# Narrow products of an HGRN2 head in two groups instead of six or seven, with ScalarE copies of their operands

## The chip, the cores and the metric

The kernel runs on one core of a Trainium2 chip. The metric is the device time of one execution in microseconds (us): the median of repeated runs on the chip. Beside it stands one execution taken by the hardware profiler; every row below is from that one. TensorE is called PE here, VectorE DVE, ScalarE ACT, GpSimd POOL, and SyncE, which issues the DMAs, SP.

## The reference

Two layers of a hybrid decoder work on 512 prompt tokens and 8 samples of 4 tokens (T = 544 columns), width 1024. Layer 0 is block-sparse attention beside a convolution; the change leaves it as it is. Layer 1 is a gated linear recurrence (HGRN2) with 8 heads of 128 keys and 128 values:

```python
q, fz, i, g = _split(h @ w_in, C_SPLITS)
f = lb + (1.0 - lb) * jax.nn.sigmoid(fz.astype(jnp.float32))
kk = (1.0 - f)
qq = jax.nn.silu(q.astype(jnp.float32))
o, S = _hgrn2_scan(qq, kk, logf, vv, S0)
o = _rms(o, o_g)
return x + (o * jax.nn.silu(g)) @ w_out, S
...
decay = jnp.exp(jnp.where(causal, diff, -jnp.inf))
a = jnp.einsum('bhtk,bhsk,bhtsk->bhts', qc, kc, decay)
o = o_inter + jnp.einsum('bhts,bhsv->bhtv', a, vc)
S = (jnp.exp(b_last)[..., None] * S + jnp.einsum('bhsk,bhsv->bhkv', kc * jnp.exp(b_last - b), vc))
```

## The kernel before

**The wide part.** `proj(hd)` computes four column tiles of a head's projection (f and q, then v and the gate g), each in two halves of 272 columns. `unit` (lines 138 to 147) does one half: 8 blocks of the input by three passes (L142, L143, L144) that add the products of high and low parts into one PSUM bank, so 24 matmuls of 128x272 in a unit and 192 in a head: the wide matmuls. Weights come by SP's DMA into `wr`; ACT rounds them to the high part `wh` (L133) and DVE takes the remainder `wl` (L134). There are three banks with the tag "g". A unit needs one, and so waits until ACT or DVE has evacuated the unit three before it: f and v by ACT (L715, L736), q and the gate by ACT's sigmoid and a DVE product (L721 with L727, L732 with L733).

**The narrow part.** `scan(hd)` is the recurrence by doubling. On level hsz = 1, 2, ... 64 the older half of each block is multiplied with the younger half, and DVE then scales both by running products of f, in place. The products use only part of PE's array: 32x80 (L781, L783) from `qx` and `kk`, 32x56 (L823) from `qy` and `kk`, 16x16 (L839), 32x32 and 64x64 (L851) from `qq` and `kk`, and 32x128 (L910) from the samples' old state `S0`, which SP loads. Their results are copied by DVE (L786, L789, L827) and ACT (L843, L856) into the matrices AD, AS and AT. After that come transposes on PE (L102), the outputs `o` (L900, L902), their squares on ACT (L931, L933), a chain of short DVE steps that makes the inverse root (L109 to L115), the normed output `on` (L937), its five transposes, the gated product `gn` (L947), and its high and low parts `oh` (L105, ACT) and `ol` (L106, DVE), which the final projection reads.

**What sets the order.** The program is traced head by head (`drain`); heads 6 and 7 run side by side. A scheduler then moves each engine's instructions, so that on PE the narrow work of a head lies between wide matmuls of the next. Each engine takes its own list in order. `tc.issue_after` keeps instructions behind another one. Buffers with a tag are handed out in program order, and a new owner waits for the last reader of the old one. Tiles from `mtile` share 16 slots with the tag "m"; before, these hold `oh` and `ol` of the eight heads, while `gg` (the gate), `vT` (the raw values) and `gn` have buffers of their own.

Of the kernel before, what the change touches and what calls it, by code (L numbers as in the profile page):

```python
# [18 lines left out]
KT = 8  # L19
# [47 lines left out]
def hybrid_step(ctx, tc, xt_in, cache_kt, cache_v, conv_in, hgrn_in, page_table, par_in, k_norm_0,  # L67
# [595 lines left out]
    with tc.tile_pool(name="l1", bufs=1) as lp:  # L663
# [32 lines left out]
        oh = [mtile(("oh", k)) for k in range(KT)]  # L696
        ol = [mtile(("ol", k)) for k in range(KT)]
# [12 lines left out]
        def proj(hd):  # L710
            f, kk, qq = mk(lp, "f", [128, T], 2), mk(lp, "kk", [128, T], 2), mk(lp, "qq", [128, TP], 2)
            gg, vT = mk(lp, "gg", [128, T], 2), mk(lp, "vT", [128, T], 2)
# [4 lines left out]
            qx = mk(lp, "qx", [128, T // 32, 80], 1)  # L717
# [45 lines left out]
        def scan(hd, f, kk, qx, qq, vt, vs, vx, gg):  # L763
# [13 lines left out]
            pl = bank("s", 400)  # L777
            for c in range(4):
                for j in range(4):
                    t0 = c * 128 + j * 32  # L780
                    PE.matmul(pl[32 * j:32 * j + 32, c * 80:c * 80 + 80], kk[:, t0:t0 + 32], qx[:, t0 // 32],  # L781
                              start=True, stop=True, tile_position=(0, 32 * j))
            PE.matmul(pl[0:32, 320:400], kk[:, TP:T], qx[:, TP // 32], start=True, stop=True, tile_position=(0, 0))  # L783
            for l in range(4):
                m = lvm[:, 32 * l:32 * l + 32].rearrange("p (g t) -> p g t", t=4)[:, :, l:]
                V.copy_predicated(ad.rearrange("p c (g t) -> p c g t", t=4)[:, :, :, l:],  # L786
                                  m.unsqueeze(1).to_broadcast([128, 4, 8, 4 - l]),
                                  lag(pl[:, :320].rearrange("p (c x) -> p c x", c=4), l))
                V.copy_predicated(as_[:TS, :TS].rearrange("p (n g t) -> p n g t", n=1, t=4)[:, :, :, l:], m[:32].unsqueeze(1),  # L789
                                  lag(pl[:32, 320:400].unsqueeze(1), l))  # L790
# [10 lines left out]
            def quads(kk, tot):  # L801
                t4 = tot[:, :TP // 4].rearrange("p (n h j) -> p n h j", h=2, j=4)

                def by(l, j, n):
                    return t4[:, :, :, j:j + n].unsqueeze(4).to_broadcast([128, 16, 2, n, 4])

                q = qy[:, :16]
                for l in (2, 3):
                    n = 4 - l
                    V.tensor_tensor(blk_lag(q, l).rearrange("p n h (j t) -> p n h j t", t=4),  # L810
                                    blk_lag(q, l - 1)[:, :, :, 4:].rearrange("p n h (j t) -> p n h j t", t=4),
                                    by(l, 1, n), op=ALU.mult)
                qo = qq.rearrange("p (n h j t) -> p n h j t", h=2, j=4, t=4)
                qi = q[:, :, 0:32].rearrange("p n (h j t) -> p n h j t", h=2, t=4)
                G.tensor_copy(qo[:, :, :, 0], qi[:, :, :, 0])
                for l in range(1, 4):
                    V.tensor_tensor(qo[:, :, :, l], blk_lag(q, l)[:, :, :, 0:4],
                                    t4[:, :, :, 0:1].to_broadcast([128, 16, 2, 4]), op=ALU.mult)
                pl = bank("s", 224)
                for c in range(4):  # L820
                    for j in range(4):
                        t0 = c * 128 + j * 32
                        PE.matmul(pl[32 * j:32 * j + 32, c * 56:c * 56 + 56], kk[:, t0:t0 + 32], qy[:, t0 // 32],  # L823
                                  start=True, stop=True, tile_position=(0, 32 * j))
                for l in range(1, 4):
                    m = lvm[:, 32 * l + 96:32 * l + 128].rearrange("p (h x) -> p h x", h=2)[:, :, 4 * l:]
                    V.copy_predicated(ad.rearrange("p c (h x) -> p c h x", h=2)[:, :, :, 4 * l:],  # L827
                                      m.unsqueeze(1).to_broadcast([128, 4, 2, 16 - 4 * l]),
                                      blk_lag(pl.rearrange("p (c x) -> p c x", c=4), l))

            while hsz < 128:
                if hsz == 4:
                    quads(kk, tot)
                if hsz == 16:
                    pl = bank("s", 64)
                    for c in range(4):
                        for j in range(4):
                            s0 = c * 128 + j * 32
                            PE.matmul(pl[32 * j:32 * j + 16, c * 16:c * 16 + 16], kk[:, s0:s0 + 16], qq[:, s0 + 16:s0 + 32],  # L839
                                      start=True, stop=True, tile_position=(0, 32 * j))  # L840
                    for j in range(4):
                        r = slice(32 * j, 32 * j + 16)
                        A.activation(ad[r, :, 16:32], pl[r].rearrange("p (c t) -> p c t", c=4), AF.Copy)  # L843
                elif hsz > 16:
                    pl = bank("s")
                    nb, w = 128 // (2 * hsz), 2
                    for c in range(4):
                        for b2 in range(nb):
                            s0 = c * 128 + b2 * 2 * hsz
                            p0 = b2 * 64 + (c % w) * hsz  # L850
                            PE.matmul(pl[p0:p0 + hsz, c * hsz:(c + 1) * hsz], kk[:, s0:s0 + hsz],  # L851
                                      qq[:, s0 + hsz:s0 + 2 * hsz], start=True, stop=True, tile_position=(0, p0))
                    for b2 in range(nb):
                        for cw_ in range(w):
                            s0, p0 = b2 * 2 * hsz, b2 * 64 + cw_ * hsz
                            A.activation(at[s0:s0 + hsz, cw_::w, s0 + hsz:s0 + 2 * hsz],  # L856
                                         pl[p0:p0 + hsz, :4 * hsz].rearrange("p (c t) -> p c t", c=4)[:, cw_::w], AF.Copy)
# [45 lines left out]
            S0 = mk(lp, "S0", [128, NS, 128], 2)  # L903
            SP.dma_start(S0, hgrn_in[hd])
            pos = bank("s", 128)
            PE.matmul(pos, as_, vs, start=True, stop=False)
            p4 = bank("t", 128)
            for b2 in range(2):
                for j in range(4):
                    PE.matmul(p4[32 * j:32 * j + 32, :], qs[:, b2], S0[:, 2 * j + b2], start=(b2 == 0), stop=(b2 == 1),  # L910
                              tile_position=(0, 32 * j))
            c4 = mk(lp, "c4", [128, 128], 1)
            A.activation(c4, p4, AF.Copy)
# [26 lines left out]
            gn = mk(lp, "gn", [128, T], 1)  # L940
# [18 lines left out]
        for _ in range(4):  # L959
# [72 lines left out]
```

## Time and profile before

| | |
|---|---|
| time, median of 3 runs | 668.96 us (668.12 to 669.68) |
| the profiled execution: its time, its span | 672.1 us, 670.3 us |
| mean granted clock of PE | 0.987 |
| PE busy (share of the span) | 642.5 us (96%), 5806 instructions |
| PE weight loads busy | 584.0 us (87%) |
| DVE busy | 519.8 us (78%) |
| ACT busy | 350.9 us (52%) |
| POOL busy | 67.5 us (10%) |
| chain of work that ended last | PE 87%, DVE 6%, DMA 2%, ACT 2% |

The span runs from the first to the last instruction, and the execution's own time has 1.8 us around it. An engine's busy time counts overlapping instructions once. The chain is followed back from the last instruction, at each step to what released it. Layer 1 starts at about 345 us; its projections begin at 356.9 us.

### The profile page before, as it was taken

What the parts mean: (1) busy time and instruction counts of PE and PEld (TensorE: products, weight loads), DVE (VectorE), ACT (ScalarE), POOL (GpSimd) and SP (SyncE); (2) the same over time, 40 slices, a digit from 0 to 9 for tenths busy, and PEclk for the clock granted to TensorE, in tenths of its full rate; (3) what the DMA queues carried; (4) which work ended last, traced back from release to release, by engine and by line L of the source; (5) the groups of instructions that cost most, each with busy time, mean ns of one, the idle gap of its engine ahead of it and who ended that gap; (6) DMA issues with size and microseconds to landing.
All of it is one profiled execution on the core that took longest, in us unless ns stands there. A gap on an engine that the chain in (4) does not pass through costs nothing.

```text
span 670.3 us, 14835 instructions
## 1 busy us (share of the span) xinstructions
PE 642.5 (96%) x5806; PEld 584.0 (87%) x5806; DVE 519.8 (78%) x1238; ACT 350.9 (52%) x866; POOL 67.5 (10%) x95
## 2 busy tenths in 40 slices
PE   8799999979898999899998999999999999999997
PEld 6799999958777976557998999999999999999997
DVE  6999999899945974544896976978787878777656
ACT  7333445638557879533665455545454545435441
POOL 6000110000101100000001210202020202020100
PEclk8999999999989999999998999999999999999999
DMA  9421343121211060575453113141313131322114
GB/s 259 161 84 64 99 141 112 39 90 65 79 49 32 32 208 1 193 238 179 141 180 132 65 64 132 64 131 64 132 64 131 64 131 65 115 75 65 73 56 145
DMA packets 34583, 70.56 MB, mean 105 GB/s; under 512 B 7378, under 2 KB 16082, under 8 KB 34514
## 3 DMA queue, kind: packets, MB, share of 16 engines
q1 hardware_dynamic: 34514, 69.62, 31.7%
q8 instruction: 45, 0.74, 0.5%
q14 instruction: 24, 0.20, 0.1%
HBM read 59.88 MB, written 9.73 MB: 104 GB/s over the span
## 4 chain that ended last, share of the span: by engine, by line
PE 87%; DVE 6%; DMA 2%; ACT 2%; issue 1%; SPq 1%; POOL 0%; DVEq 0%
PE g L142 23%; PE g L144 22%; PE g L143 22%; PE t L102 4%; PE s L470 2%; DVE m L516 2%; PE o L493 1%; PE s L622 1%; DMA kn<-in_cache_kt_dram 1%; PE t L887 1%; PE o L900 1%; PE s L781 1%; PE o L902 1%; PE s L587 1%; DMA xTall<-in_xt_dram 1%
## 5 line engine op out<-in xcount | busy, mean ns | idle before, releaser
L142 PE MATMUL g<-h,wh 128*128 128x272 f32 x944 | 278.2, 295 | 8.5 <-ACT f L715 2.6
L143 PE MATMUL g<-h,wh 128*128 128x272 f32 x944 | 276.4, 293 | 2.0 <-DVE h L273 2.0
L144 PE MATMUL g<-h,wl 128*128 128x272 f32 x944 | 275.0, 292 | 0.0
L142 PEld LDWEIGHTS g<-h,wh 128*128 128x128 f32 x944 | 179.8, 191 | 12.8 <-ACT f L715 3.1
L143 PEld LDWEIGHTS g<-h,wh 128*128 128x128 f32 x944 | 179.6, 190 | 3.3 <-DVE h L273 2.5
L144 PEld LDWEIGHTS g<-h,wl 128*128 128x128 f32 x944 | 179.7, 190 | 1.1 <-issue 0.8
L133 ACT ACTIVATE wh<-wr 128x1024 fp32r<-128x1024 f32 (+4 forms) x90 | 88.2, 982 | 96.8 <-PE g L143 85.2
L134 DVE TENSOR_TENSOR wl<-wr,wh 128x1024 fp32r<-128x1024 f32 (+4 forms) x90 | 108.0, 1201 | 37.1 <-ACT wh L133 37.0
L516 DVE SCALAR_TENSOR_TENSOR m<-m,vecs,m 128x512 f32<-128x512 f32 x120 | 83.9, 732 | 0.1
L143 PE MATMUL g<-m,wh 128*128 128x272 f32 x256 | 74.3, 292 | 0.0
L142 PE MATMUL g<-m,wh 128*128 128x272 f32 x256 | 74.0, 298 | 0.1
L144 PE MATMUL g<-m,wl 128*128 128x272 f32 x256 | 74.0, 291 | 0.0
L142 PEld LDWEIGHTS g<-m,wh 128*128 128x128 f32 x256 | 47.5, 190 | 6.8 <-issue 3.6
L143 PEld LDWEIGHTS g<-m,wh 128*128 128x128 f32 x256 | 48.2, 188 | 2.2 <-DVE mx L598 0.8
L144 PEld LDWEIGHTS g<-m,wl 128*128 128x128 f32 x256 | 48.2, 188 | 0.4 <-issue 0.2
L478 DVE TENSOR_REDUCE mx<-s 128x1 f32<-128x128 f32 (+3 forms) x32 | 15.4, 482 | 15.5 <-PE s L472 15.5
L470 PE MATMUL s<-kz,qT 128*128 128x128 f32 (+3 forms) x64 | 23.5, 451 | 0.3 <-ACT PP L481 0.2
L916 ACT ACTIVATE S<-S,tot 128x128 f32<-128x128 f32 x64 | 20.4, 390 | 4.8 <-PE t L910 4.8
L865 DVE TENSOR_TENSOR kk<-kk,tot 128x256 f32<-128x256 f32 (+1 forms) x48 | 21.8, 454 | 0.0
L918 POOL TENSOR_TENSOR ve<-vx,cst 128x1024 fp32r<-128x1024 f32 x8 | 15.5, 1942 | 62.4 <-DVE vx L708 45.5
L971 DVE TENSOR_TENSOR xTall<-g,xTall 128x272 f32<-128x272 f32 x32 | 13.4, 436 | 8.4 <-PE g L144 8.0
L481 ACT ACTIVATE PP<-s,mx,rq 128x128 f32<-128x128 f32 (+3 forms) x32 | 19.6, 612 | 0.2
(292 smaller groups left out, 981.6 us busy)
## 6 DMA issues: line engine op xcount, KB each, us to landing
wr<-in_w_in_dram SPq DMA_DIRECT2D x58, 512.0 KB, 3.5
wr<-in_w_out_dram SPq DMA_DIRECT2D x16, 512.0 KB, 3.6
kn<-in_cache_kt_dram SPq DMA_DIRECT2D x16, 256.0 KB, 3.3
kn<-in_cache_v_dram SPq DMA_DIRECT2D x16, 256.0 KB, 4.3
S<-in_hgrn_dram SPq DMA_DIRECT2D x8, 512.0 KB, 3.6
out_hgrns_dram<-S SPq DMA_DIRECT2D x8, 512.0 KB, 3.3
xTall<-in_xt_dram SPq DMA_DIRECT2D x8, 272.0 KB, 5.4
out_y_dram<-xTall SPq DMA_DIRECT2D x8, 272.0 KB, 2.1
```

The source lines that it names most:

```text
L102: PE.transpose(out, in_, ident[:np_, :np_])
L133: A.activation(wh, raw, AF.Copy)
L134: V.tensor_tensor(wl, raw, wh, op=ALU.subtract)
L142: PE.matmul(ps, wh[:, k - k0, :], ah, start=(k == k0), stop=False)
L143: PE.matmul(ps, wh[:, k - k0, :], al, start=False, stop=False)
L144: PE.matmul(ps, wl[:, k - k0, :], ah, start=False, stop=(k == k1 - 1))
L470: PE.matmul(ss[hh][:, :L], qT[:, i * 128:(i + 1) * 128], kT[:, hh, 0:L], start=True, stop=False)
L481: A.activation(P[:, :L], s[:, :L], AF.Exp, bias=mx[:, 1:2], scale=rqc, accum_out=mx[:, 2:3])
L516: V.scalar_tensor_tensor(cy[c][:, :TP], up[c][:, j:j + TP], cw[:, c, j:j + 1], cy[c][:, :TP], op0=ALU.mult, op1=ALU.add)
L865: V.tensor_tensor(k3[:, :, 0, :], k3[:, :, 0, :], t3[:, :, 1:2].to_broadcast([128, nblk, hsz]), op=ALU.mult)
L916: A.activation(S0[:, n], S0[:, n], AF.Copy, scale=tots[:, n:n + 1])
L918: G.tensor_tensor(ve, vx.unsqueeze(1).to_broadcast([128, NS, 128]), exm.unsqueeze(2).to_broadcast([128, NS, 128]), op=ALU.mult)
```

## The change

Narrow products: a head has two groups now. The first, at hsz = 4 (L810 to L831), holds the 32x56 products (L818), behind them the 32x80 products (L824, L826) and the products with the old state (L829). The second, at hsz = 64 (L855 to L872), holds the 64x64 (L859), the 32x32 (L865) and the 16x16 products (L869). Operands that have been overwritten by then are kept by ACT copies with the tag "kv" (two buffers): 1-f of 544 columns (L783), and for hsz 16 and 32 the older half of `kk` and the younger half of `qq`, 256 columns each (L851, L852): five copies in a head, 40 in all. `qx` has two buffers, and `S0` is loaded before the first group (L780). The heads 6 and 7 are joined after six steps of head 6 instead of four.

Buffers: `gg` and `vT` come from the 16 slots "m"; `gn` is written over `gg` (L960); `oh` and `ol` are taken for a head when it is done, that of the last head from the tag "f".

```diff
-        oh = [mtile(("oh", k)) for k in range(KT)]
-        ol = [mtile(("ol", k)) for k in range(KT)]
+        oh, ol = [None] * KT, [None] * KT
...
-            gg, vT = mk(lp, "gg", [128, T], 2), mk(lp, "vT", [128, T], 2)
+            gg, vT = mtile(("gg", hd), F32), mtile(("vT", hd), F32)
-            qx = mk(lp, "qx", [128, T // 32, 80], 1)
+            qx = mk(lp, "qx", [128, T // 32, 80], 2)
...
+            S0 = mk(lp, "S0", [128, NS, 128], 2)
+            SP.dma_start(S0, hgrn_in[hd])
+            c4 = mk(lp, "c4", [128, 128], 1)
+            kv = mk(lp, "kv", [128, T], 2)
+            A.activation(kv, f, AF.Copy, scale=-1.0, bias=1.0)
+            def behind(ins):
+                return tc.issue_after(ins.ins)
...
                 pl = bank("s", 224)
+                pf = bank("s", 400)
+                p4 = bank("t", 128)
-                        PE.matmul(pl[...], kk[:, t0:t0 + 32], qy[:, t0 // 32], ...)
+                        last = PE.matmul(pl[...], kk[:, t0:t0 + 32], qy[:, t0 // 32], ...)
+                with behind(last):
+                            PE.matmul(pf[...], kv[:, t0:t0 + 32], qx[:, t0 // 32], ...)
+                    PE.matmul(pf[0:32, 320:400], kv[:, TP:T], qx[:, TP // 32], ...)
+                            PE.matmul(p4[...], qs[:, b2], S0[:, 2 * j + b2], ...)
+                A.activation(c4, p4, AF.Copy)
...
+                if hsz in (16, 32):
+                    old = mk(lp, "kv", [128, T], 2)[:, :TP].rearrange("p (a n t) -> p a n t", a=2, t=hsz)
+                    A.activation(old[:, 0], kk[...][:, :, 0], AF.Copy)
+                    A.activation(old[:, 1], qq[...][:, :, 1], AF.Copy)
+                    olds.append(old)
+                if hsz == 64:
+                    k16, k32 = olds
+                            last = PE.matmul(pl[...], kk[:, s0:s0 + 64], qq[:, s0 + 64:s0 + 128], ...)
+                    with behind(last):
+                                PE.matmul(pl[...], k32[:, 0, 2 * c + b2], k32[:, 1, 2 * c + b2], ...)
+                                PE.matmul(pl[...], k16[:, 0, 4 * c + j], k16[:, 1, 4 * c + j], ...)
...
-                V.scalar_tensor_tensor(gn[:, sl], p, vec("on"), gg[:, sl], op0=ALU.mult, op1=ALU.mult)
+                V.scalar_tensor_tensor(gg[:, sl], p, vec("on"), gg[:, sl], op0=ALU.mult, op1=ALU.mult)
+            oh[hd] = mtile(("oh", hd))
+            ol[hd] = mtile(("ol", hd)) if hd < KT - 1 else mk(lp, "f", [128, T], 2, F32R)
             for sl in (slice(0, 256), slice(256, T)):
-                split(oh[hd][:, sl], ol[hd][:, sl], gn[:, sl])
+                split(oh[hd][:, sl], ol[hd][:, sl], gg[:, sl])
...
-        for _ in range(4):
+        for _ in range(6):
             next(s6)
```

**Place A, the end of head 0.** PE before: `o_4739` is head 0's output, `s_5132` takes head 1's first products, `t_4804` and `t_4809` the transposes of head 0's normed output; g are wide matmuls. Left out are wide matmuls alone, in the first gap 30 of them and in the second 21.

```order
L902 MATMUL o_4739<-S_4733,qq_4279 128x128
L922 MATMUL t_4776<-ve_4771,kts_4721 128x512
L823 MATMUL s_5132<-qy_5087,kk_4819 32x56 x16
L144 MATMUL g_5363<-h_81,wl_5334 128x272
...
L839 MATMUL s_5158<-qq_4820,kk_4819 16x16 x16
...
L142 MATMUL g_5418<-h_83,wh_5333 128x272
L102 MATMUL t_4804<-cst,on_4799 128x128 x4
L102 MATMUL t_4809<-cst,ons_4800 128x128
L143 MATMUL g_5418<-h_91,wh_5333 128x272
```

PE now (`o_4742`, `s_5102`, `t_4793` and `t_4798` are the same things):

```order
L925 MATMUL o_4742<-S_4736,qq_4263 128x128
L143 MATMUL g_5003<-h_95,wh_4939 128x272
L144 MATMUL g_5003<-h_87,wl_4940 128x272
L818 MATMUL s_5102<-qy_5078,kk_4810 32x56 x16
L102 MATMUL t_4793<-cst,on_4789 128x128 x4
L102 MATMUL t_4798<-cst,ons_4790 128x128
L824 MATMUL s_5103<-qx_4814,kv_5088 32x80 x16
L826 MATMUL s_5103<-qx_4814,kv_5088 32x80
L142 MATMUL g_5029<-h_80,wh_4945 128x272
```

The transposes of the normed output stood 59 rows behind the last output matmul; now two wide matmuls and the first products stand between them. On ACT the list there is now (`sq` and `sd`: the norm's squares and sums of head 0; `m_4264` is the gated output, `m_4813` head 1's raw values, which L735 evacuates from a wide bank):

```order
L852 ACTIVATE kv_5164<-qq_4811 128x256
L947 ACTIVATE sq_4770,sd_4771<-o_4742 128x128
L133 ACTIVATE wh_5331<-wr_5329 128x1024
L947 ACTIVATE sq_4770,sd_4771<-o_4742 128x128 x3
L851 ACTIVATE kv_5164<-kk_4810 128x256
L105 ACTIVATE m_4803<-m_4264 128x256
L735 ACTIVATE m_4813<-g_4949 128x272
L735 ACTIVATE m_4813<-g_5003 128x272
```

A weight rounding (L133) stands between the first and the other three squares.

**Place B, heads 2 to 5, here where head 3 ends while head 4 is projected.** PE before: first products, transposes of head 3's output, 16x16 products with transposes between them, 32x32 products, each between wide matmuls (only wide ones are left out, but for the last transpose of the output):

```order
L144 MATMUL g_6866<-h_86,wl_6837 128x272
L823 MATMUL s_6635<-qy_6590,kk_6322 32x56 x16
L142 MATMUL g_6866<-h_87,wh_6836 128x272
...
L142 MATMUL g_6895<-h_81,wh_6830 128x272
L102 MATMUL t_6307<-cst,on_6302 128x128 x4
...
L144 MATMUL g_6895<-h_86,wl_6831 128x272
L839 MATMUL s_6661<-qq_6323,kk_6322 16x16 x9
L102 MATMUL t_6572<-cst,vT_6325 128x128 x4
L102 MATMUL t_6581<-cst,r_6579 128x128
L839 MATMUL s_6661<-qq_6323,kk_6322 16x16 x7
...
L144 MATMUL g_6921<-h_87,wl_6837 128x272
L851 MATMUL s_6686<-qq_6323,kk_6322 32x32 x8
L142 MATMUL g_6962<-h_80,wh_6952 128x272
```

PE now: the first group with the five transposes inside, and the second group.

```order
L144 MATMUL g_6527<-h_87,wl_6464 128x272
L818 MATMUL s_6626<-qy_6602,kk_6334 32x56 x16
L102 MATMUL t_6317<-cst,on_6313 128x128 x4
L102 MATMUL t_6322<-cst,ons_6314 128x128
L824 MATMUL s_6627<-qx_6338,kv_6612 32x80 x16
L826 MATMUL s_6627<-qx_6338,kv_6612 32x80
L142 MATMUL g_6553<-h_80,wh_6469 128x272
...
L143 MATMUL g_6859<-h_92,wh_6849 128x272
L859 MATMUL s_6702<-qq_6335,kk_6334 64x64 x4
L865 MATMUL s_6702<-kv_6695 32x32 x8
L829 MATMUL t_6628<-S_6609,QS_4245 32x128 x8
L869 MATMUL s_6702<-kv_6688 16x16 x16
L927 MATMUL s_6782<-VS_4244,AS_4243 128x128
```

Products that stood apart stand together; the wide matmul behind L826, `g_6553`, is the first of a unit, and its bank is the one of `g_6473`.

**Place C, the same place on ACT and DVE.** ACT before (`gn` to `m` is the output rounding, `vT` the evacuation of the values):

```order
L133 ACTIVATE wh_6836<-wr_6834 128x1024
L736 ACTIVATE vT_6325<-g_6515 128x272
L916 ACTIVATE S_6250<-S_6250,tot_6126 128x128 x6
...
L931 ACTIVATE sq_6283,sd_6284<-s_6252 128x128
L933 ACTIVATE sq_6283,sd_6284<-o_6242 128x128 x4
L715 ACTIVATE f_6822<-g_6840 128x272
L721 ACTIVATE sg_6891<-g_6866 128x272
L105 ACTIVATE m_4264<-gn_6306 128x256
L105 ACTIVATE m_4264<-gn_6306 128x288
```

ACT now (`m_6327` is head 3's `oh`, `m_5828` its gated output, `m_6337` head 4's raw values, from the banks `g_6473` and `g_6527`):

```order
L852 ACTIVATE kv_6688<-qq_6335 128x256
L133 ACTIVATE wh_6855<-wr_6853 128x1024
L105 ACTIVATE m_6327<-m_5828 128x256
L735 ACTIVATE m_6337<-g_6473 128x272
L735 ACTIVATE m_6337<-g_6527 128x272
L105 ACTIVATE m_6327<-m_5828 128x288
```

DVE now (`m_5828` is the gated output again, `wl_6856` the remainder of `wh_6855`):

```order
L888 TENSOR_TENSOR kk_6334<-kk_6334,tot_6618 128x64x4
L134 TENSOR_TENSOR wl_6856<-wr_6853,wh_6855 128x1024
L960 SCALAR_TENSOR_TENSOR m_5828<-t_6317,vecs,m_5828 128x256 x2
L960 SCALAR_TENSOR_TENSOR m_5828<-t_6322,vecs,m_5828 128x32
L888 TENSOR_TENSOR kk_6334<-kk_6334,tot_6683 128x32x8
```

The evacuation of the values stood ten rows ahead of the output rounding, and stands directly behind its first piece now; the piece reads what DVE writes behind the remainder of the weights that ACT rounded one row earlier.

## Rows read from the trace of the kernel before

**Rows 1.** Windows view, projections of layer 1: busy time (count) by engine, PEclk, DMA.

```profile
365.00:656.00 291.00, 291.00 (x3171) 275.92 (x3170) 223.34 (x663) 141.15 (x430) 37.64 (x46) 1.00 0.26 87
```

**Rows 2.** Timeline, PE: start, us, line; narrow stretches alone, then two joined.

```profile
480.27 0.29 PE L144 MATMUL g<-h,wl 128*128 128x272 f32 x1
480.49 0.60 PE L823 MATMUL s<-qy,kk 128*32 128x56 f32 x32
481.25 0.29 PE L143 MATMUL g<-h,wh 128*128 128x272 f32 x1
...
455.84 0.33 PE L851 MATMUL s<-qq,kk 128*32 128x32 f32 x16
456.33 0.29 PE L143 MATMUL g<-h,wh 128*128 128x272 f32 x1
...
641.93 0.64 PE L910 MATMUL t<-S,QS 128*32 128x128 f32 x16
642.73 0.29 PE L142 MATMUL g<-m,wh 128*128 128x272 f32 x1
...
619.06 0.64 PE L910 MATMUL t<-S,QS 128*32 128x128 f32 x16
619.52 0.31 PE L851 MATMUL s<-qq,kk 128*32 128x32 f32 x16
619.99 0.29 PE L142 MATMUL g<-m,wh 128*128 128x272 f32 x1
```

**Rows 3.** Timeline, PE: 64-wide products alone, then joined to the first products.

```profile
625.14 0.45 PE L851 MATMUL s<-qq,kk 128*64 128x64 f32 x8
625.76 0.29 PE L142 MATMUL g<-m,wh 128*128 128x272 f32 x1
...
611.32 0.45 PE L851 MATMUL s<-qq,kk 128*64 128x64 f32 x8
611.71 0.60 PE L823 MATMUL s<-qy,kk 128*32 128x56 f32 x32
612.47 0.29 PE L143 MATMUL g<-m,wh 128*128 128x272 f32 x1
```

**Rows 4.** Timeline, ACT: a weight rounding, two norm squares, an output rounding.

```profile
487.33 1.06 ACT L133 ACTIVATE wh<-wr 128x1024 fp32r<-128x1024 f32 x1
...
474.51 0.28 ACT L933 ACTIVATE sq<-o 128x128 f32<-128x128 f32 x1
474.91 0.28 ACT L933 ACTIVATE sq<-o 128x128 f32<-128x128 f32 x1
...
483.16 0.42 ACT L105 ACTIVATE m<-gn 128x256 fp32r<-128x256 f32 x1 [1.06 <-DVE gn L947]
```

**Rows 5.** Timeline, DVE: a weight remainder, three steps of the root, gated product.

```profile
526.79 1.21 DVE L134 TENSOR_TENSOR wl<-wr,wh 128x1024 fp32r<-128x1024 f32 x1
...
476.20 0.15 DVE L109 TENSOR_SCALAR sd<-sd 128x5 f32<-128x5 f32 x1
477.52 0.14 DVE L114 SCALAR_TENSOR_TENSOR sd<-sd 128x5 f32<-128x5 f32 x1
479.11 0.69 DVE L937 TENSOR_TENSOR on<-o,sd 128x512 f32<-128x512 f32 x1
...
482.65 0.48 DVE L947 SCALAR_TENSOR_TENSOR gn<-t,vecs,gg 128x256 f32<-128x256 f32 x1
```

**Rows 6.** Windows view: three idle stretches of PE, each with what followed.

```profile
171.80:176.00 4.20, 2.71 (x22) 2.67 (x22) 4.15 (x10) 3.70 (x7) 0.00 (x0) 1.00 0.00 0
...
183.20:185.80 2.60, 0.82 (x7) 0.53 (x6) 1.80 (x4) 1.64 (x3) 0.00 (x0) 1.00 0.41 156
185.80:188.60 2.80, 2.80 (x12) 2.80 (x13) 2.44 (x5) 0.00 (x0) 0.00 (x0) 0.50 0.36 100
...
354.20:356.90 2.70, 0.05 (x2) 0.01 (x1) 2.52 (x5) 2.67 (x5) 2.15 (x12) 0.92 0.57 164
356.90:359.60 2.70, 2.70 (x12) 2.70 (x13) 2.14 (x7) 1.73 (x3) 0.00 (x0) 0.50 0.90 338
```

More of the change, by code (lines that the diff above doesn't have):

```diff
@@ L776, in scan @@
                 V.tensor_tensor(q4[:, :, :, l], lag(qx, l)[:, :, :, 0], f4[:, :, :, 0], op=ALU.mult)
[L777 to L790, printed above, removed]
             for b2 in range(2):
@@ L822, in quads @@
                         t0 = c * 128 + j * 32
-                        PE.matmul(pl[32 * j:32 * j + 32, c * 56:c * 56 + 56], kk[:, t0:t0 + 32], qy[:, t0 // 32],
-                                  start=True, stop=True, tile_position=(0, 32 * j))
+                        last = PE.matmul(pl[32 * j:32 * j + 32, c * 56:c * 56 + 56], kk[:, t0:t0 + 32], qy[:, t0 // 32],
+                                         start=True, stop=True, tile_position=(0, 32 * j))
+                with behind(last):
+                    for c in range(4):
+                        for j in range(4):
+                            t0 = c * 128 + j * 32
+                            PE.matmul(pf[32 * j:32 * j + 32, c * 80:c * 80 + 80], kv[:, t0:t0 + 32], qx[:, t0 // 32],
+                                      start=True, stop=True, tile_position=(0, 32 * j))
+                    PE.matmul(pf[0:32, 320:400], kv[:, TP:T], qx[:, TP // 32], start=True, stop=True, tile_position=(0, 0))
+                    for b2 in range(2):
+                        for j in range(4):
+                            PE.matmul(p4[32 * j:32 * j + 32, :], qs[:, b2], S0[:, 2 * j + b2], start=(b2 == 0),
+                                      stop=(b2 == 1), tile_position=(0, 32 * j))
+                A.activation(c4, p4, AF.Copy)
+                for l in range(4):
+                    m = lvm[:, 32 * l:32 * l + 32].rearrange("p (g t) -> p g t", t=4)[:, :, l:]
+                    V.copy_predicated(ad.rearrange("p c (g t) -> p c g t", t=4)[:, :, :, l:],
+                                      m.unsqueeze(1).to_broadcast([128, 4, 8, 4 - l]),
+                                      lag(pf[:, :320].rearrange("p (c x) -> p c x", c=4), l))
+                    V.copy_predicated(as_[:TS, :TS].rearrange("p (n g t) -> p n g t", n=1, t=4)[:, :, :, l:], m[:32].unsqueeze(1),
+                                      lag(pf[:32, 320:400].unsqueeze(1), l))
                 for l in range(1, 4):
@@ L833, in scan @@
                     quads(kk, tot)
-                if hsz == 16:
-                    pl = bank("s", 64)
-                    for c in range(4):
[L837 to L840, printed above, removed]
+                if hsz in (16, 32):
+                    old = mk(lp, "kv", [128, T], 2)[:, :TP].rearrange("p (a n t) -> p a n t", a=2, t=hsz)
+                    A.activation(old[:, 0], kk[:, :TP].rearrange("p (n s t) -> p n s t", s=2, t=hsz)[:, :, 0], AF.Copy)
+                    A.activation(old[:, 1], qq.rearrange("p (n s t) -> p n s t", s=2, t=hsz)[:, :, 1], AF.Copy)
+                    olds.append(old)
@@ new lines, in scan @@
+                if hsz == 64:
+                    k16, k32 = olds
+                    pl = bank("s")
+                    for c in range(4):
+                        s0, p0 = c * 128, (c % 2) * 64
+                        last = PE.matmul(pl[p0:p0 + 64, 192 + c * 64:256 + c * 64], kk[:, s0:s0 + 64],
+                                         qq[:, s0 + 64:s0 + 128], start=True, stop=True, tile_position=(0, p0))
+                    with behind(last):
+                        for c in range(4):
+                            for b2 in range(2):
+                                p0 = b2 * 64 + (c % 2) * 32
+                                PE.matmul(pl[p0:p0 + 32, 64 + c * 32:96 + c * 32], k32[:, 0, 2 * c + b2],
+                                          k32[:, 1, 2 * c + b2], start=True, stop=True, tile_position=(0, p0))
+                        for c in range(4):
+                            for j in range(4):
+                                PE.matmul(pl[32 * j:32 * j + 16, c * 16:c * 16 + 16], k16[:, 0, 4 * c + j],
+                                          k16[:, 1, 4 * c + j], start=True, stop=True, tile_position=(0, 32 * j))
@@ L841, in scan @@
                     for j in range(4):
                         r = slice(32 * j, 32 * j + 16)
[L843 to L857, printed above, removed]
+                        A.activation(ad[r, :, 16:32], pl[r, :64].rearrange("p (c t) -> p c t", c=4), AF.Copy)
@@ new lines, in scan @@
+                    for hz, o in ((32, 64), (64, 192)):
+                        for b2 in range(64 // hz):
+                            for cw_ in range(2):
+                                s0, p0 = b2 * 2 * hz, b2 * 64 + cw_ * hz
+                                A.activation(at[s0:s0 + hz, cw_::2, s0 + hz:s0 + 2 * hz],
+                                             pl[p0:p0 + hz, o:o + 4 * hz].rearrange("p (c t) -> p c t", c=4)[:, cw_::2],
+                                             AF.Copy)
@@ L902, in scan @@
                     PE.matmul(po[:, sl], qq[:, sl], S[:, (c - 1) * 128:c * 128], start=False, stop=True)
-            S0 = mk(lp, "S0", [128, NS, 128], 2)
-            SP.dma_start(S0, hgrn_in[hd])
             pos = bank("s", 128)
             PE.matmul(pos, as_, vs, start=True, stop=False)
[L907 to L913, printed above, removed]
             PE.matmul(pos, cst[:, C_SEL2:C_SEL2 + 128], c4, start=False, stop=True)
```

2 lines of the change are left out of this document (1 added, 1 removed).

## The prediction

> **What bounds the kernel now.** I read the views in this order: busy time by stage, PE's timeline where narrow products stand, the rows of ACT and DVE that would lie in the new chains, and PE's idle stretches with the clock behind them. In the projections of layer 1 PE is busy for 291.00 of 291 us, at the full clock [rows 1]. DVE has 223 us of work there, ACT 141, POOL 38, and the DMA engines are busy for 0.26. So whatever PE is spared here is gained, as long as nothing else makes it wait; no row of this stage has PE waiting, so every wait that the change adds is paid in full. Layer 0 keeps its order on every engine.
>
> **What the grouping saves.** A wide matmul takes about 0.125 us: 22 of them in 2.71 us of work at full clock [rows 6]. A narrow stretch costs more than its own products, since PE goes over to it and back. From the last wide start to the narrow start there are 0.22 us (480.27 to 480.49) [rows 2]. From the narrow start to the second wide start behind it there are 0.49 us for the 32x32 products, 0.80 for those with the old state, and 0.93 for both in one stretch. Less the two wide cadences that lie in each of these distances (0.25), the first two cost 0.46 and 0.77, 1.23 together, and the joined stretch 0.90: a join at the same width saves 0.33. Where the width changes inside the stretch, 64 wide and then 32 wide, the same sum is 0.59 and 0.73 apart, against 0.73 + 0.39 = 1.12 joined [rows 2, 3]: a join saves 0.20 there, so the change of width keeps 0.13.
>
> By the order of layer 1, 58 narrow stretches become 32, and the changes of width inside a stretch go from one to eight. That is 26 x 0.33 - 7 x 0.13 = 7.7 us less on PE. If each change of width ate the whole saving, it would be 19 x 0.33 = 6.3; if it ate nothing, 8.6. I take 7.7, as measured, and keep both ends. The Trainium skill (TensorEngine Tiling (Array Packing), Key Properties) says that a change of tiling mode, not just of tile, drains TensorE, which would make every change of width cost like a return to the wide matmuls; by that rule alone the saving is the lower end, 6.3. The trace agrees that a change of width costs something, but shows 0.13, less than half of 0.33.
>
> **What is added at nothing.** 40 ACT copies: 32 of 256 columns, 0.42 each as the output rounding of that size [rows 4], and 8 of 544, about twice that: 20 us of ACT beside its 141 in 291. They are hidden, but for what stands behind them in ACT's list; the chains below contain that. `S0` is loaded earlier, ahead of two weight loads on SP, with DMA busy for 0.26; and `qx` has a second buffer, so the earlier product of the next head needs no wait. The second group waits for DVE's scaling up to hsz = 32; between the two groups lie 38 wide matmuls, 4.7 us, and the 1.9 of the first group itself, beside about as much DVE work. I put no wait there, with 0 to 1 us per head as bounds: this is the thinnest cover.
>
> **The new wait at the end of head 0 (place A).** PE now has the transposes of head 0's output directly behind head 1's first products, which start two wide matmuls after the last output product. Count from the start of these products. ACT has done the first square; then comes a weight rounding of 1.06, and the other three squares at 0.40 each (474.51 to 474.91) [rows 4]: 2.3 us. DVE takes the weight remainder of 1.21 meanwhile. The chain of short steps took 2.9 from its first step to the start of the normed output, of which 1.6 are the eight steps from 477.52 on; other copies lay between the first three [rows 5]. I take 2.5 (2.2 without anything between, 2.9 as seen). The normed output takes 0.69. So the transposes can start at 2.3 + 0.1 + 2.5 + 0.7 = 5.6, and PE is through the first products at 0.5: it waits 5.1 us. In the order of before 53 wide matmuls behind the first products, 6.6 us, covered this. Behind the transposes the chain of the next paragraph adds 0.5: 5.6 us in all, 5.2 to 6.2.
>
> **The new wait in heads 3 to 6 (places B, C).** The unit behind L826 needs the bank of the values' first half. ACT evacuates that bank behind the first piece of the previous head's output rounding, and ACT takes its list in order. That piece needs the gated product, which on DVE stands behind the remainder of weights that ACT rounds last before, and ACT can start that rounding only when the unit ahead of the first products is through, since its buffer is still read until then. Counted again from the start of the first products: rounding 1.06, remainder 1.21, gated product 0.48, output rounding 0.42 [rows 4, 5], evacuation about the same 0.4, less some overlap: 3.5. PE has, until then, the first products (0.5), five transposes at no more than a wide one's 0.125 (0.6), and 17 products of 80 columns with the return, as the 16 of 128 (0.8) [rows 2]: 1.9. It waits 1.6 us, 1.3 to 2.0. The order is alike in the projections of heads 3, 4, 5 and 6: 6.4 us. For head 2 the remainder stands behind the gated product, the wait is about 0.2. Before, the evacuation stood ten rows ahead of the output rounding, and no row showed the wait.
>
> **The clock.** PE idle for 2.7 us was followed by 2.7 us at a granted clock of 0.50, which is 1.2 instead of 2.4 GHz: 12 wide matmuls in place of 21 [rows 6], 1.35 us lost. The wait of 5.1 us should do this once. After 1.6 us with little work the clock stayed at 1.00 (171.80 to 176.00); after 2.6 us with 0.82 busy it fell to 0.50. The waits of 1.6 lie behind a second and more of narrow work and transposes, between these two rows; I take no fall there.
>
> **The sum.** -7.7 + 5.6 + 0.2 + 6.4 + 1.35 = +5.9 us. The profiled execution took 672.1 us, with a span of 670.3, so it would be 678.0 there; the median of the runs shown is 3.1 lower, and on it I forecast 668.96 + 5.9 = 674.9. About 0.2%, 1.3 us, is what a measurement of this kernel can tell from no change.
>
> **The rivals.**
> - *The clock falls in heads 3 to 6 too.* For it speaks the window with 0.82 of 2.6 us busy [rows 6]; against it, that narrow products keep PE busy here. It adds 4 x 1.35 = 5.4: 680.3. A chance of 0.2.
> - *Only the wait at the end of head 0 bites.* If the values are evacuated in time in heads 3 to 6 (the rounding of the weights starting earlier than its list and buffer let me read), 6.4 us go: 668.5, no change. 0.08.
> - *No new wait: faster.* If the chains behind both waits end before PE is through, only the saving is left: 668.96 - 7.7 = 661.3. For it speaks that DVE and ACT have idle time in every head [rows 1]. It decides at place A: the chain would have to end within 0.5 us of the first products instead of 5.6, which needs the squares to run well ahead of them; the list of ACT speaks against it, since the last output matmul comes only two wide ones before. 0.07.
> - *DVE is late for the second group*, by about 1 us in six heads: 681. 0.07. It looks like the forecast with one more wait per head.
> - The forecast itself, with the bounds of its terms (671 to 678): 0.58.
>
> **How the numbers follow.** The likeliest is 674.9. The range takes the forecast's bounds and most of the clock's case: 669.8 to 681.0. It leaves out the fast case, half of the unchanged one and what lies above. Faster by over 0.2%: the third case and little else, 0.08. Within 0.2%: the second, 0.09. Slower: 0.83.
>
> **What would show it.** In the profile of the changed kernel PE should be idle for about 5 us once, near 390 to 410 us, released by DVE's normed output, with a clock of 0.50 in the 2.7 us behind it. It should be idle for 1.6 us once a head in four heads, in front of an L142, released by ACT's L735. From first products to first products a head in between should take as long as before, within 0.3 us. Narrow stretches should cost 1.1 to 1.2 us for the group of three or four. I am wrong if PE stays busy through these places, or if the idle time lies in front of L859 instead.

## The result, and the profile after

The changed kernel takes 678.0 us (median of 4 runs, 674.98 to 679.43), the kernel before 669.32 in the same comparison: a ratio of 1.0126, 95% interval 1.0083 to 1.0169. The forecast was 674.9 (669.8 to 681.0), slower with a chance of 0.83. The profiled execution took 676.65 us, with a span of 674.7. The page's busy times and chain:

```profile
span 674.7 us, 14874 instructions
PE 637.5 (94%) x5806; PEld 584.9 (87%) x5806; DVE 514.5 (76%) x1238; ACT 363.3 (54%) x906; POOL 64.8 (10%) x95
...
PE 84%; DVE 5%; ACT 5%; DMA 4%; issue 1%; SPq 1%; POOL 0%; DVEq 0%; ACTq 0%; POOLq 0%
```

PE is busy for 5 us less than before, in a span that is 4.4 us longer, and its share of the chain fell from 87% to 84%. The view of waits, PE's from 360 us on (engine, line, what it waited for; us in total, times, the longest):

```profile
PE g L142 <- ACT m L735: 5.7, 5, 1.4
PE t L102 <- DVE on L951: 5.4, 1, 5.4
```

Before, there was no such row in this stage [rows 1]. Ahead of it, in every kernel here, PE waits for 2.65 us at the layer boundary; three units of head 0's projection stand in front of that wait (from 344.6 us on before, 342.8 now), so the 356.9 us given above for the start of the projections is the end of this wait. Up to there PE's order is the same in all kernels. The large one stands at place A. PE's timeline there:

```profile
399.55 0.39 PE L925 MATMUL o<-S,qq 128*128 128x128 f32 x2
...
400.12 0.60 PE L818 MATMUL s<-qy,kk 128*32 128x56 f32 x32
406.11 1.11 PE L102 MATMUL t<-cst,on 128*128 128x128 f32 x4 [5.39 <-DVE on L951]
407.02 0.42 PE L102 MATMUL t<-cst,ons 128*128 128x128 f32 x1
407.36 1.30 PE L824 MATMUL s<-qx,kv 128*32 128x80 f32 x32
408.43 0.47 PE L826 MATMUL s<-qx,kv 128*32 128x80 f32 x2
408.84 0.60 PE L142 MATMUL g<-h,wh 128*128 128x272 f32 x1
```

Head 1's first products start at 400.12; the transposes of head 0's output start at 406.11, after 5.39 us without work. The granted clock (the column behind the five busy times) in that wait and behind it, windows view:

```profile
400.70:406.10 5.40, 0.02 (x4) 0.00 (x0) 4.80 (x17) 2.06 (x8) 0.00 (x0) 0.81 0.55 209
406.10:409.20 3.10, 3.09 (x40) 2.54 (x41) 2.02 (x7) 1.42 (x5) 0.49 (x3) 0.50 0.37 148
409.20:412.00 2.80, 2.80 (x18) 2.80 (x18) 2.74 (x13) 0.51 (x2) 0.15 (x1) 0.70 0.00 0
```

It falls to 0.50 behind the wait: the four transposes take 1.11 us on the timeline and the products of 80 columns 1.30, against 0.66 and 0.76 at the full clock in the next rows. The other waits stand at place B. PE's timeline there, in the projection of head 3:

```profile
473.18 0.60 PE L818 MATMUL s<-qy,kk 128*32 128x56 f32 x32
473.72 0.66 PE L102 MATMUL t<-cst,on 128*128 128x128 f32 x4
...
474.41 0.76 PE L824 MATMUL s<-qx,kv 128*32 128x80 f32 x32
474.99 0.30 PE L826 MATMUL s<-qx,kv 128*32 128x80 f32 x2
476.67 0.39 PE L142 MATMUL g<-h,wh 128*128 128x272 f32 x1 [1.38 <-ACT m L735]
```

The timeline of ACT in the same stretch:

```profile
473.17 1.06 ACT L133 ACTIVATE wh<-wr 128x1024 fp32r<-128x1024 f32 x1 [1.70 <-PE g L143]
475.91 0.42 ACT L105 ACTIVATE m<-m 128x256 fp32r<-128x256 f32 x1 [1.69 <-DVE m L960]
476.24 0.67 ACT L735 ACTIVATE m<-g 128x272 f32<-128x272 f32 x2
```

And that of DVE:

```profile
474.26 1.23 DVE L134 TENSOR_TENSOR wl<-wr,wh 128x1024 fp32r<-128x1024 f32 x1
475.40 1.03 DVE L960 SCALAR_TENSOR_TENSOR m<-t,vecs,m 128x256 f32<-128x256 f32 x3
```

The rounding of weights starts with the first products (473.17), the remainder follows at 474.26, the gated product at 475.40, the output rounding at 475.91 and the values' evacuation at 476.24; PE waits for it from 475.29 to 476.67. The chain is the one of the prediction, link by link.

### The profile page after: what moved, and what is told of

Read it like the earlier page. It is cut to its first block, busy times and chain, and to the rows that moved or that the text cites. A ratio compares the mean times of both kernels' runs of the same rounds, so it can differ in the third digit from the quotient of the medians.

```text
span 674.7 us, 14874 instructions
## 1 busy us (share of the span) xinstructions
PE 637.5 (94%) x5806; PEld 584.9 (87%) x5806; DVE 514.5 (76%) x1238; ACT 363.3 (54%) x906; POOL 64.8 (10%) x95
## 4 chain that ended last, share of the span: by engine, by line
PE 84%; DVE 5%; ACT 5%; DMA 4%; issue 1%; SPq 1%; POOL 0%; DVEq 0%; ACTq 0%; POOLq 0%
PE g L142 22%; PE g L143 22%; PE g L144 22%; PE t L102 4%; PE s L470 2%; DMA kn<-in_cache_kt_dram 2%; PE o L493 2%; PE s L622 1%; DVE wl L134 1%; ACT wh L133 1%; DMA wr<-in_w_in_dram 1%; PE o L923 1%; PE t L910 1%; PE o L925 1%; DMA xTall<-in_xt_dram 1%
## 5 line engine op out<-in xcount | busy, mean ns | idle before, releaser
L133 ACT ACTIVATE wh<-wr 128x1024 fp32r<-128x1024 f32 (+4 forms) x90 | 88.2, 982 | 130.2 <-PE g L143 118.7
L134 DVE TENSOR_TENSOR wl<-wr,wh 128x1024 fp32r<-128x1024 f32 (+4 forms) x90 | 100.9, 1123 | 20.9 <-ACT wh L133 20.0
L142 PE MATMUL g<-m,wh 128*128 128x272 f32 x256 | 73.7, 295 | 0.0
L143 PE MATMUL g<-m,wh 128*128 128x272 f32 x240 | 69.4, 291 | 0.0
L142 PEld LDWEIGHTS g<-m,wh 128*128 128x128 f32 x256 | 47.4, 188 | 5.8 <-issue 3.8
L143 PEld LDWEIGHTS g<-m,wh 128*128 128x128 f32 x240 | 45.2, 188 | 2.0 <-DVE mx L598 0.8
L888 DVE TENSOR_TENSOR kk<-kk,tot 128x256 f32<-128x256 f32 (+1 forms) x48 | 25.2, 526 | 2.5 <-PE s L818 2.4
L488 ACT ACTIVATE PT<-t 128x128 f32<-128x128 f32 (+3 forms) x32 | 13.7, 433 | 14.6 <-PE t L102 14.5
```

The lines of the kernel that those rows point to most:

```text
L133: A.activation(wh, raw, AF.Copy)
L134: V.tensor_tensor(wl, raw, wh, op=ALU.subtract)
L142: PE.matmul(ps, wh[:, k - k0, :], ah, start=(k == k0), stop=False)
L143: PE.matmul(ps, wh[:, k - k0, :], al, start=False, stop=False)
L888: V.tensor_tensor(k3[:, :, 0, :], k3[:, :, 0, :], t3[:, :, 1:2].to_broadcast([128, nblk, hsz]), op=ALU.mult)
```

## The experiments

**1. One step traced later.** The split of a head's output into `oh` and `ol`, the first writes of two slots of the ring, is traced behind the next head's projection. The work is the same.

```diff
+            if hd < 6:
+                yield
             oh[hd] = mtile(("oh", hd))
...
-        for hd in range(6):
-            drain(scan(hd, *proj(hd)))
-        s6 = scan(6, *proj(6))
+        prev = None
+        for hd in range(7):
+            cur = scan(hd, *proj(hd))
+            if prev is not None:
+                drain(prev)
+            if hd == 6:
+                break
+            for _ in range(10):
+                next(cur)
+            prev = cur
+        s6 = cur
```

> Only the place of one step in the traced order differs from the change: the split of a head's gated output into oh and ol (the first write of two slots of the ring) is traced behind the next head's projection, so the ring's slots are handed to the next head's gate and values first. Theory (the waits come from the order in which the ring's slots are handed out): the four waits of 1.4 us in front of the unit behind the 80-column products and the wait of 5.4 us at the end of head 0 are gone, the clock does not fall between 390 and 420 us, and the saving on PE of 6.3 to 8.6 us is left: 660 to 663 us, faster than both kernels. Rival (the waits come from the grouping itself, whose chains on ACT and DVE are too long for the time PE leaves them): the waits stay, 674 to 679 us. Rival (the grouping saves nothing on PE): no waits and 668 to 670 us.

Measured: 663.27 us (662.27 to 665.08), ratio to before 0.9921 (0.9895 to 0.9948). The start of one head's first products and of the next head's, PE's timeline of the changed kernel:

```profile
506.95 0.60 PE L818 MATMUL s<-qy,kk 128*32 128x56 f32 x32
...
540.78 0.60 PE L818 MATMUL s<-qy,kk 128*32 128x56 f32 x32
```

The same of this kernel:

```profile
435.61 0.60 PE L818 MATMUL s<-qy,kk 128*32 128x56 f32 x32
...
467.96 0.60 PE L818 MATMUL s<-qy,kk 128*32 128x56 f32 x32
```

33.83 and 32.35 us: 1.48 less, of which 1.38 is the wait. The stretch from 365 to 645 us in the windows view of the changed kernel (busy times of PE, PE's weight loads, DVE, ACT, POOL; clock):

```profile
365.00:645.00 280.00, 268.89 (x3027) 259.20 (x3026) 206.62 (x630) 150.72 (x460) 34.69 (x46) 0.99 0.26 86
```

And of this one:

```profile
365.00:645.00 280.00, 279.96 (x3137) 271.27 (x3135) 222.51 (x657) 154.11 (x470) 38.06 (x46) 1.00 0.29 89
```

Both kinds of waits are gone, the one at head 0 too: with the ring's slots free for head 1, the scheduler puts the output's transposes 54 rows behind the first products. The first theory held; the time is 0.3 us above its range.

**2. The values in a buffer of their own.** `vT` leaves the ring, the gate stays.

```diff
-            gg, vT = mtile(("gg", hd), F32), mtile(("vT", hd), F32)
+            gg, vT = mtile(("gg", hd), F32), mk(lp, "vT", [128, T], 1)
...
-            sq = mk(lp, "sq", [128, 128], 2)
+            sq = mk(lp, "sq", [128, 128], 1)
```

> The change, but the raw values have a buffer of their own (one) outside the ring; the gate stays in the ring. (The squares' scratch has one buffer instead of two, to make room.) Theory: the evacuation of the values no longer stands behind the output rounding on ACT, so the four waits of 1.4 us in front of the unit behind the 80-column products go, and with them the order that put the output's transposes directly behind the first products at head 0; some shorter waits may come where the gate, still in the ring, stands behind ol on DVE: 661 to 667 us. Rival (the ring is not the cause): 674 to 679 us with the same waits.

Measured: 669.66 us (667.9 to 671.65), ratio to before 1.0005 (0.9981 to 1.003), above the range of 661 to 667. PE's largest wait from 360 us on (the rest are three of 0.14):

```profile
PE g L142 <- ACT f L714: 2.9, 6, 0.5
```

The waits for L735 and for the normed output are gone, as the theory has it. Another came in their place: 0.5 us in six heads, 2.9 in all, for the evacuation of f. The order also leaves 35 narrow stretches where the first experiment has 30. From the wait at the layer boundary to the last wide matmul this kernel takes 308.8 us, the first experiment 302.4; of these 6.4, 3.3 are waits and by the prediction's prices 1.4 are stretches (five more, two changes of width fewer). The rest is not explained.

**3. The whole end of a head traced later** (squares, root, transposes, gated product and split): as in the first experiment, with nine steps ahead instead of ten and no `yield` before the split.

> As the first run, but the whole last part of a head (squares, root, transposes of the output, gated product and split) is traced behind the next head's projection. Theory: no waits either; but the narrow products are left in more stretches by the order (46 against 30), so less is saved: 16 x 0.33 = 5.3 us less at most, some of them joined with transposes: 661 to 667 us. Rival (waits come from the chain of the root): a wait in front of the output's transposes stays at some heads.

Measured: 665.84 us (664.19 to 668.0), ratio 0.9952 (0.993 to 0.9974), and PE without a wait behind the layer boundary. The median is 2.6 above the first experiment, for 16 more narrow stretches; from the wait at the boundary to the last wide matmul the profiles differ by 4.2 (306.6 against 302.4). The 5.3 that these stretches would cost at most were an upper bound.

**4. The ring alone.** The kernel before, with gate, values, `oh` and `ol` in the ring as in the change; narrow products as before, no copies.

```diff
...
-            gg, vT = mk(lp, "gg", [128, T], 2), mk(lp, "vT", [128, T], 2)
+            gg, vT = mtile(("gg", hd), F32), mtile(("vT", hd), F32)
...
-                V.scalar_tensor_tensor(gn[:, sl], p, vec("on"), gg[:, sl], op0=ALU.mult, op1=ALU.mult)
+                V.scalar_tensor_tensor(gg[:, sl], p, vec("on"), gg[:, sl], op0=ALU.mult, op1=ALU.mult)
+            oh[hd] = mtile(("oh", hd))
+            ol[hd] = mtile(("ol", hd)) if hd < KT - 1 else mk(lp, "f", [128, T], 2, F32R)
```

> The kernel before with one part of the change alone: gate, values, oh and ol share the ring, oh and ol taken for a head when it is done; the narrow products stay as before, with no copies. Theory: the ring's order alone makes PE wait, in every head and by at least the 1.4 us a head that the changed kernel shows, and as nothing is saved it is slower than the changed kernel: over 677 us. Rival (the ring is harmless and the grouping brings the waits): 668 to 671 us with PE busy through layer 1.

Measured: 702.09 us (699.13 to 704.88), ratio 1.0489 (1.0444 to 1.0534): 33 us slower than before, much more than the least that was expected. PE's waits from 360 us on (the longest of those left out is 1.7 us):

```profile
PE g L142 <- ACT m L735: 8.1, 6, 2.2
PE s L822 <- DVE sd L114: 6.3, 2, 3.1
PE t L102 <- DVE on L936: 2.5, 2, 2.2
...
PE s L850 <- ACT AT L855: 1.6, 1, 1.6
```

Its stretch from 365 to 645 us in the windows view:

```profile
365.00:645.00 280.00, 256.95 (x2758) 243.00 (x2756) 191.02 (x587) 121.97 (x366) 31.29 (x45) 0.94 0.26 81
```

The wait for L735 stands in six heads, 8.1 us. Others came with it, most of them for DVE (steps of the root, the normed output, copies into AD), in front of narrow products and transposes; what holds these up was not traced. All waits together are 23 us. The mean clock of the stretch is 0.94, which is some 34 of its 280 us at half clock, and that comes on top. So the ring by itself makes waits, without any grouping.

**5. The changed kernel three times more**, a profile of each.

> The changed kernel once more, to see what differs between its executions, which spread from 675.0 to 679.4 us. Theory: the waits are the same to 0.1 us in each (5.4 us once, 1.4 us four times, released by the normed output and by the values' evacuation), and what differs is TensorE's clock behind them: in a slow execution it falls to 1.2 GHz behind one or more of the 1.4 us waits too, about 1.35 us each. Rival: the clock falls only behind the 5.4 us wait, and the spread lies in layer 0, ahead of 357 us.

> As e5_change_again_1: the waits alike to 0.1 us; what differs is either the clock behind the 1.4 us waits (theory) or layer 0 (rival).

> As e5_change_again_1: the waits alike to 0.1 us; what differs is either the clock behind the 1.4 us waits (theory) or layer 0 (rival).

Measured: 673.84, 674.47 and 675.86 us. With the changed kernel's first profile there are four. The waits are the same in all: 5.38 to 5.39 us once, 1.37 to 1.38 four times, 0.18 to 0.19 once. The clock fell behind none of the sixteen waits of 1.4 us, and behind the 5.4 us in each profile. Windows view of the first of the three, idle time and what followed, at the layer boundary and at a wait of 1.4 us:

```profile
350.30:353.00 2.70, 0.05 (x2) 0.02 (x1) 2.53 (x5) 2.67 (x5) 2.16 (x12) 1.00 0.57 117
353.00:356.00 3.00, 3.00 (x24) 3.00 (x25) 2.44 (x7) 1.72 (x3) 0.00 (x0) 1.00 0.94 380
471.00:472.50 1.50, 0.12 (x2) 0.06 (x1) 1.50 (x6) 0.82 (x3) 0.00 (x0) 1.00 0.38 41
472.50:475.00 2.50, 2.50 (x20) 2.50 (x21) 2.50 (x13) 1.54 (x5) 0.80 (x2) 1.00 0.49 185
```

The same of the third, at the layer boundary alone:

```profile
350.00:352.70 2.70, 0.10 (x1) 0.00 (x0) 2.47 (x5) 2.67 (x5) 2.16 (x12) 1.00 0.55 121
354.40:357.30 2.90, 2.90 (x14) 2.90 (x14) 1.87 (x6) 0.28 (x2) 0.00 (x0) 0.50 0.63 253
```

The theory fell. Two things about the clock differ in these profiles. At the layer boundary 2.65 us of idle time were followed by half clock in two of the four executions (the changed kernel's first profile and the third here) and by the full clock in the other two. And behind the 5.4 us wait the half clock lasted 4.8 and 5.0 us in the same two, 3.3 and 3.2 us in the others. Windows view of the first of the three, whose wait ends at 402.62:

```profile
402.60:405.90 3.30, 3.28 (x41) 2.72 (x42) 2.22 (x7) 1.60 (x6) 0.65 (x3) 0.50 0.40 161
405.90:409.00 3.10, 3.10 (x27) 3.10 (x26) 2.76 (x14) 0.57 (x3) 0.00 (x0) 1.00 0.00 0
```

Together they make 2.2 us: from the wait at the boundary to the last wide matmul there are 316.1 us in both of the first kind, 313.9 in both of the second. The rest of the spread lies ahead of that stretch, which starts between 352.8 and 355.0 us, and behind it (3.6 to 5.3 us), so the rival held in part. The executions over 679 us were not among the profiled ones. Their mean granted clock is 0.980, against 0.982 to 0.990 in the four profiles, so a part of their time may be the clock; where it fell, and what else made them slower, stays open.

**6. Every copy twice.** The first experiment's kernel with the 40 copies of old operands issued a second time, to the same place.

```diff
             A.activation(kv, f, AF.Copy, scale=-1.0, bias=1.0)
+            A.activation(kv, f, AF.Copy, scale=-1.0, bias=1.0)
...
                     A.activation(old[:, 0], kk[...][:, :, 0], AF.Copy)
+                    A.activation(old[:, 0], kk[...][:, :, 0], AF.Copy)
+                    A.activation(old[:, 1], qq[...][:, :, 1], AF.Copy)
                     A.activation(old[:, 1], qq[...][:, :, 1], AF.Copy)
```

> The first experiment's kernel with each of the 40 copies of old operands made twice, 20 us of work more on ScalarE. Theory (the copies are hidden where no order makes TensorE wait for them): as the first experiment, 663 us within 1.5, and TensorE without a wait in layer 1. Rival (ScalarE is close to being the limit there): a wait in each head, 0.5 us or more, 666 us or more.

Measured: 662.0 us (659.94 to 664.6), ratio 0.9885 (0.9839 to 0.9932). The stretch from 365 to 645 us:

```profile
365.00:645.00 280.00, 279.36 (x3135) 271.09 (x3134) 221.72 (x655) 168.78 (x508) 35.81 (x45) 1.00 0.28 89
```

ACT is busy for 14.7 us more than in the first experiment (168.78 against 154.11), and PE for 0.6 us less: one wait of 0.64 us for ACT (L901) stands at 599.8 us, against the expectation of none. The time is not longer for it; but for this wait the copies are hidden.

**7. The ring with the later split, without the grouping.** The fourth experiment's kernel with the edit of the first.

> The ring alone (fourth experiment) with the split traced later as in the first experiment; the narrow products stay as before, with no copies. Theory: the ring costs nothing once the order in which its slots are handed out is mended, so TensorE has no wait in layer 1 and the time is that of the kernel before, 667.5 to 670.5 us; the 6 us that the first experiment is faster are then the grouping's alone. Rival (the later split gains by itself): 661 to 665 us. Rival (the ring keeps a cost): over 672 us.

Measured: 669.26 us (667.97 to 671.08) beside 669.27 for the kernel before, ratio 1.0002 (0.9983 to 1.002). The same stretch:

```profile
365.00:645.00 280.00, 280.00 (x3082) 265.01 (x3081) 215.67 (x635) 140.02 (x426) 36.58 (x45) 1.00 0.27 87
```

No wait, and no gain: PE is busy throughout, in 58 narrow stretches as before, so the ring with its order mended and the later split together cost and gain nothing. What the first experiment gains is then the grouping's, together with the join of heads 6 and 7 after six steps of head 6 instead of four, which the first experiment has and this kernel has not; no run takes these two apart.

**8. Heads 6 and 7 joined later.** The first experiment's kernel, where nine steps of head 6 are traced ahead of the last projection instead of six.

```diff
-        for _ in range(6):
+        for _ in range(9):
             next(s6)
```

> The first experiment's kernel, with heads 6 and 7 joined after nine steps of head 6 instead of six, a trial for a faster version. Theory: fewer narrow stretches are cut apart between these two heads, three or four at 0.33 us: 1 us less than the first experiment, 660.5 to 664 us. Rival (the end of head 6 comes too late and the last projection waits): 665 us or more, with a wait of TensorE behind 600 us.

Measured: 658.79 us (658.68 to 661.47), ratio 0.9846 (0.9819 to 0.9873), below the expected range and faster than every other kernel here. PE has no wait behind the layer boundary. From the wait there to the end of the last wide matmul the profile has 298.9 us (352.5 to 651.4), the first experiment's 302.4 (355.1 to 657.6). That is 3.5 less, but the first experiment's profile had 16 wide matmuls at half clock at the boundary and this one none, about 1.5. So the later join brings some 2.0 us in these profiles, twice what was expected: the order leaves 24 narrow stretches instead of 30, not three or four fewer, and 6 x 0.33 is 2.0. The spans of the two profiles are 4.1 apart; what is not explained of that is the time ahead of the boundary (same order, 2.6 us shorter here) and behind the last matmul (2.0 longer).

## Why the prediction was right

**The bound and the saving.** PE was the limit and stayed it. The saving was forecast as 26 x 0.33 - 7 x 0.13 = 7.7 us. From the wait at the layer boundary to the end of the last wide matmul the kernel before has 309.8 us (356.9 to 666.7) and the first experiment 302.4: 7.4 less, with the clock falling at the boundary in both (12 and 16 wide matmuls at half clock, which alone is 0.2 against the first experiment). That neither the ring nor the later split gives it is shown by the seventh experiment (309.9 us, 353.1 to 663.0). The first experiment's order is not quite the forecast one: it leaves 30 narrow stretches with ten changes of width instead of 32 with eight, for which the same prices give 28 x 0.33 - 9 x 0.13 = 8.1 us. The rule of the Trainium skill (TensorEngine Tiling (Array Packing), Key Properties), read as a full price for every change of width, would have given 6.3 for both orders; 7.4 to 7.6 is nearer to the joins as read from the rows, but below them. What was wrong is the size of a group: I wrote 1.1 to 1.2 us for three or four kinds together. The second group, PE's timeline:

```profile
482.17 0.45 PE L859 MATMUL s<-qq,kk 128*64 128x64 f32 x8
482.55 0.33 PE L865 MATMUL s<-kv 128*32 128x32 f32 x16
482.69 0.63 PE L829 MATMUL t<-S,QS 128*32 128x128 f32 x16
483.13 0.50 PE L869 MATMUL s<-kv 128*16 128x16 f32 x32
...
483.81 0.37 PE L144 MATMUL g<-h,wl 128*128 128x272 f32 x1
```

It takes 1.39 us from 482.17 to 483.56, where the products of the next step begin, and the way into it comes on top. The error changed no term of the sum, which counts joins.

**The wait at the end of head 0.** Forecast 5.1 us in front of the output's transposes and 0.5 behind them, 5.6; measured 5.39 and none. The first part is longer because the first step of the root starts 0.45 us behind the last square (402.86), not 0.1; a scaling of `kk` stands before it on DVE. The second part fell away: at half clock PE's own work, from the transposes to the next wide matmul, lasts 2.7 us (406.11 to 408.84) instead of the 1.4 counted, and the evacuation, which starts at 408.10, comes in time.

**The waits in heads 3 to 6.** Forecast 4 x 1.6; measured 4 x 1.38 = 5.5. PE goes on 3.5 us behind the start of the first products (473.18 to 476.67), as counted; but its own work lasts 2.1 of that (to 475.29), not 1.9. Head 2: 0.2 forecast, 0.18 measured. From first products to first products a head takes 33.83 us against 33.71 before (480.49 to 514.20), as forecast within 0.3.

**The clock.** Forecast 1.35 us. In the first profile the half clock lasts from 406.1 to about 410.9 (0.50 up to 409.2, 0.70 over the next 2.8 us), not 2.7 us. The 60 matmuls from the transposes on take 6.37 us there; the same 60 at the full clock, in the projection of head 3, take 5.68 with a wait of 1.38, so 4.30 of work: 2.1 us lost. In the profiles of experiment 5 the same sum gives 1.4, 1.4 and 2.2. So the term came out as forecast in two executions and was 0.7 to 0.8 too small in the other two; the 2.7 us of the prediction is the width of one window of [rows 6], and the length of the half clock is not always the same. That the clock would stay up behind the short waits was right, in all sixteen of the four profiles. The rival by which it falls there too, 680.3 us, does not hold in them; for the two executions over 679 us it is not excluded.

**The sum.** In the profiles the stretch grew from 309.8 to 316.1 us (355.0 to 671.1), by 6.3, against +5.9 forecast. Of it 5.4 + 0.2 + 5.5 are waits, 2.1 the clock behind the large one and 0.2 the boundary, 13.4 together; so what is left for the saving in this order is 7.1, where 7.7 was forecast. The sum comes as close as it does partly by luck, since errors cancel: the short waits were forecast 0.9 longer than they are and the clock's cost 0.7 smaller, and the saving 0.6 larger. The medians are 8.7 apart, with an interval of 5.6 to 11.3 (0.0083 and 0.0169 of 669.3). All seven executions of the changed kernel, with those of experiment 5, have a median of 675.86, 6.5 above 669.32; so the four of the result lie on the long side. The wait at the layer boundary, ahead of which the order is the same everywhere, ended between 352.5 and 356.9 us in the profiles of this study, so a part of the difference of the medians may lie there.

**The cause behind the waits.** The prediction gave the order of ACT's and DVE's lists as the cause and read it from the orders. Experiments 1, 2, 4 and 7 show what makes that order: slots of a shared ring are handed out in traced order, `oh` and `ol` of a head stand ahead of the next head's gate and values, and those may not be written before. Neither the grouping nor the copies bring such a wait. The rival with full gain named about the time of a kernel without waits (661.3; the first experiment has 663.3), but it asked for faster chains in the same order, and what took the waits away was another order.

## What to carry to other kernels

A ring of buffers that several producers share is also an order: a buffer taken late for one stage, ahead of early ones of the next stage, ties an evacuation to the end of a long chain, and a saturated engine pays for each such tie in full. Before a change that saves buffers and time together is judged, its two parts are worth running apart; here the saving was 7.4 us and the sharing cost 13.7 (316.1 against 302.4), and moving one step in the traced order kept the first without the second. To forecast such a change, take the list of each engine as it now stands, find what stands ahead of each evacuation, and add up the chain from the rows.

## What the runs showed of the hardware

- The same idle time of 2.65 us at the layer boundary was followed by half clock in two executions and by the full clock in two others of the same kernel (experiment 5), and in nine of all twelve profiles; 5.4 us brought half clock in all four and 1.4 us in none of sixteen.
- Behind the wait of 5.4 us the half clock lasted 4.8 us of work in one execution (406.1 to 410.9), and 3.3, 3.2 and 5.0 in three others of the same kernel (experiment 5), longer than the 2.7 us of the window behind the layer boundary [rows 6].
- Twice the copies on ACT, 14.7 us more of its time in 280, did not lengthen the time (662.0 us against 663.3), with one wait of 0.64 us on PE (experiment 6).
